# The entry of the first feed-forward block: the norm's weight moved behind the transposes, products ordered by weight tile

## The chip, the core and the metric

The kernel runs on one core of a Trainium2 chip. The metric is the device time of one execution in microseconds (us). Before the change the median of three runs is 1098.65 us (1098.41 to 1099.42).

## What is computed

The reference sends 256 tokens of 1024 channels through a block of feed-forward, attention and feed-forward parts, and then through two more layers. Only its first step matters here, the gate and up projections of the first feed-forward part behind its norm:

```python
def _rmsnorm(x, g):
    xf = x.astype(jnp.float32)
    r = lax.rsqrt(jnp.mean(xf * xf, axis=-1, keepdims=True) + EPS)
    return (xf * r * g.astype(jnp.float32)).astype(x.dtype)

def _swiglu(x, w_gate, w_up, w_down):
    return (jax.nn.silu(x @ w_gate) * (x @ w_up)) @ w_down
...
        f = _swiglu(_rmsnorm(x, ffn1_pre_g[l]), ffn1_w_gate[l], ffn1_w_up[l], ffn1_w_down[l])
```

Everything is float32.

## The kernel before

A float32 product is made of three products of a narrower type (float32r). Each operand is split into a high part, its cast, and a low part, the rest, and high x high, high x low and low x high are added up in PSUM. For weights, `Stream` does this: `load_to` (L68) issues 512 KB tiles on SP's queue into four raw buffers (`wraw`), `copy_next` (L77) casts a tile to `wh` (on ACT at L89, or on DVE at L87) and returns a function that makes `wl` (L94) on the engine it is given; a raw buffer is free, and the next load issued, when its low part is done. `copy_next` is called in program order; every engine works through its own instructions strictly in the order written here by hand.

Tokens come in two halves of 128. For each, `ew` (L386) has the squares summed (`rms`, L327: ACT at L336, then two small POOL operations for the scale r at L344 and L346) and writes `xs` = x times r times the norm's weight (DVE, L423). `to_t` (L362) transposes it in eight 128x128 pieces on PE (L370, against the identity `ident`), copies the result out of PSUM to the high part `xh` (ACT, L373) and returns the function that makes the low part `xl` (DVE, L378).

`setup` (L275) issues the loads: the tokens' first half, three weight tiles, the second half and a fourth tile on SP's queue; the norm's weight as one row on ACT's queue; `ident` and the table of small constants `small` on POOL's queue. PE runs `WARM` = 5 products of zeros (L300), then spreads the row over 128 partitions by products with a column of ones (L304, names `grow`), and DVE reads it from PSUM.

`enter_first` (L490) orders the entry of the first block. The first projection's weights are four tiles of two 128-row pieces (`w_first`: gate and up columns side by side, 512 wide). The inner function `first` of `ffn` (L631) makes the 24 products of one token half in one PSUM bank (`fh`, L642): for each tile high x high and high x low, at the end the eight low x high. The first half's 24 products stand first, with the second half's transposes before the last four of them; then the second half's 24. Behind them `gemm_b2` (L525) begins the next stage, products named `gb` (L535, L537).

Of the kernel before, what the change touches and what calls it, by code (L numbers as in the profile page):

```python
# [32 lines left out]

NB_RAW = 4
NB_HL = 6
WARM = 5


SM = {}
_o = 0  # L40
for _n, _w in (("convw", 16), ("convb", 4), ("ba", 4), ("bx", 4), ("lam", 4), ("glub", 4),
               ("lr", 16), ("li", 16), ("ldt", 16), ("d", 16)):
    SM[_n] = (_o, _w)
    _o += _w
NSM = _o

GAINS = ("ffn1_pre_g", "ffn1_post_g", "mix_pre_g", "mix_post_g", "ffn2_pre_g", "ffn2_post_g",
         "ab_norm_2", "ffn_norm_2_0", "cd_norm_2", "ffn_norm_2_1", "final_norm_2")


class Stream:
# [53 lines left out]
    def used(self):  # L105

        self.free = self.nt

    def take(self, n, used=True):
        if used:  # L110
# [78 lines left out]
class Kern:  # L189
# [85 lines left out]
    def setup(self):  # L275
        nc, A = self.nc, self.A
        nc.scalar.preload_act_table_set("silu_and_others")
        self.x = self.const.tile([P, 2, D + 4], F32, name="x")
        nc.gpsimd.memset(self.x[:, :, D:D + 1], 32.0 * math.sqrt(EPS))

        def load_x(h):
            for c in (slice(0, 512), slice(512, D)):
                nc.sync.dma_start(out=self.x[:, h, c], in_=A["x"][128 * h:128 * h + 128, c])

        load_x(0)
        self.ws.load_to(3)
# [5 lines left out]
        nc.vector.memset(t[:, 256:384], 1.0)  # L292
        warm = t[:, 0:256].bitcast(BF16)
        g = self.pre_of(0)
# [12 lines left out]
        nc.gpsimd.dma_start(out=self.ident, in_=A["c_ident"])  # L307
        self.mhalf = self.const.tile([P, 16], F32, name="mhalf")
        nc.gpsimd.memset(self.mhalf, -0.5)
        self.small = self.const.tile([P, NSM], F32, name="small")  # L310
        nc.gpsimd.dma_start(out=self.small, in_=A["smalls"])
        if self.phases[0] != "f1":
            for _ in self.s5_powers():
                pass
            for _ in self.rg_prep():
                pass

    def sv(self, name, i=None, n=1):
        o, w = SM[name]
        return self.small[:, o:o + w] if i is None else self.small[:, o + i:o + i + n]  # L320
# [41 lines left out]
    def to_t(self, h, src, oh, ol, n=8):  # L362

        nc = self.nc
        lo = []
        for b in range(0, n, 4):
            p = self.ps("tp")
            m = min(4, n - b)
            for j in range(m):
                nc.tensor.transpose(p[:, j * P:(j + 1) * P], src[:, (b + j) * P:(b + j + 1) * P], self.ident)  # L370
            pv = p[:, :m * P].rearrange("p (a t) -> p a t", a=m)
            hv = oh[:, b:b + m, h * P:(h + 1) * P]
            nc.scalar.copy(out=hv, in_=pv)  # L373
            lo.append((ol[:, b:b + m, h * P:(h + 1) * P], pv, hv))

        def low():
            for o, pv, hv in lo:
                nc.vector.tensor_sub(out=o, in0=pv, in1=hv.bitcast(F32))  # L378

        return low  # L380

# [4 lines left out]
    def ew(self, h, gname):  # L386

        nc = self.nc
        c2 = (slice(0, 512), slice(512, D))
        xv = self.x[:, h, :]  # L390
        xs = self.tmp.tile([P, D + 4], F32, name="xs", tag="xs")

        t = self.tmp.tile([P, D + 1], F32, name="pt", tag="pt", bufs=1)
        xsq = self.rms((xv[:, 0:512], xv[:, 512:D + 1]), t, 1.0 / 32)
        accs, gpost, coef = self.fin or (None, None, None)
        if gpost:
            acc = accs[h]
# [91 lines left out]

    def enter_first(self, e0, e1, first):  # L490

        V, G = self.nc.vector, self.nc.gpsimd
        for _ in range(3):
            next(e0)
        self.ws.copy_next()(G)
        xs = next(e0)
        self.ws.copy_next(V)(V)
        next(e1)
        next(e1)
        self.new_xt()  # L500
        low = self.to_t(0, xs, self.xh, self.xl)
        split = self.ws.copy_next()
        low()
        split(V)
        next(e1)
        self.ws.copy_next()(V)
        xs = next(e1)
        self.ws.ahead = 4
        first(0, lambda: self.to_t(1, xs, self.xh, self.xl)())
        self.ws.ahead = NB_HL  # L510
        self.ws.split_to(NB_HL)
        first(1, None)


    def mm3(self, out, prods, start, stop, late=False, mid=None):
# [99 lines left out]
    def ffn(self, gpre, gpost, coef, gnext, hooks=None, cut=False):  # L615
        nc = self.nc
        tt = nc.vector.tensor_tensor
        with self.tc.tile_pool(name="ffn", bufs=3) as fp:
# [5 lines left out]
            st = {}  # L624
            accs = None

            def act(c):
                hh, hl = hts[c // 2]
                return hh[:, c % 2, :], hl[:, c % 2, :]

            def first(h, mid):  # L631
                if h == 0:
# [10 lines left out]
                sg = fp.tile([P, S], F32, name="sgf", tag="sgf", bufs=2)  # L643
                nc.scalar.activation(out=sg, in_=p[:, 0:S], func=AF.Silu)
                tt(out=sg, in0=sg, in1=p[:, S:2 * S], op=ALU.mult)
                st[h] = sg

            def split(t, j):
                hh = fp.tile([P, 2, S], F32R, name="hh", tag="hh")
# [17 lines left out]
            for j in range(1, 11):  # L667
                sg = fp.tile([P, 2, S], F32, name="sg", tag="sg", bufs=1)
# [3 lines left out]
                if j == 1:  # L672
                    p = self.ps("ft")
# [1028 lines left out]
def _layout(inputs):  # L1702

    import numpy as np
    g = {k: np.asarray(v) for k, v in inputs.items()}
    A = {n: g[n] for n in _RAW}
# [8 lines left out]
    for n in GAINS:  # L1715
# [7 lines left out]
    q, k = g["q_norm_g"][0], g["k_norm_g"][0]  # L1723
    A["gqk"] = np.stack([q, sw(q), k, sw(k)])
    ch = lambda a: a.reshape(4, P).T
    st = lambda a: a.reshape(16, 2, 64).transpose(1, 2, 0).reshape(P, 16)
# [6 lines left out]
        "d": np.tile(g["cd_d_2"][0].reshape(16, 32).T, (4, 1)),  # L1733
# [27 lines left out]
```

## Time and profile before

| | |
|---|---|
| median of three runs | 1098.65 us |
| the profiled execution, its own time | 1100.22 us |
| its span, first to last instruction | 1098.4 us |
| PE busy | 1082.7 us, 99% of the span |
| DVE, ACT, POOL busy | 738.0, 598.3, 314.6 us |
| start of the next stage's first product (L535) | 27.35 us into the span |

The page gives shares of the whole span; a change that touches the first 28 us is read from the timeline of this stretch. In a timeline row the first number is the start in us from the span's start, the second the length, then engine, line, operation and tiles; "x8" means eight of them merged, and what stands in brackets is the idle time of the engine before it and what ended that. Matmul records overlap: the pace is the distance of their starts, not their length.

### The profile page before, as it was taken

What the parts mean: (1) busy time and instruction counts of PE and PEld (TensorE: products, weight loads), DVE (VectorE), ACT (ScalarE), POOL (GpSimd) and SP (SyncE); (2) the same over time, 40 slices, a digit from 0 to 9 for tenths busy, and PEclk for the clock granted to TensorE, in tenths of its full rate; (3) what the DMA queues carried; (4) which work ended last, traced back from release to release, by engine and by line L of the source; (5) the groups of instructions that cost most, each with busy time, mean ns of one, the idle gap of its engine ahead of it and who ended that gap; (6) DMA issues with size and microseconds to landing.
All of it is one profiled execution on the core that took longest, in us unless ns stands there. A gap on an engine that the chain in (4) does not pass through costs nothing.

```text
span 1098.4 us, 16117 instructions
## 1 busy us (share of the span) xinstructions
PE 1082.7 (99%) x5963; PEld 921.1 (84%) x5963; DVE 738.0 (67%) x1019; ACT 598.3 (54%) x954; POOL 314.6 (29%) x561
## 2 busy tenths in 40 slices
PE   8999999999999999999999999999999999999997
PEld 5888888878878888888987888888889888888886
DVE  5665676889676665667764676757777557565564
ACT  4667555556556554556575554545553465554553
POOL 4005840213310000003023599999505100000000
PEclk9999999999999999999999999999999999999999
DMA  7765565562056655655713665565454346656651
GB/s 237 252 203 179 193 206 176 188 217 75 20 159 226 207 176 193 208 175 185 225 54 100 212 202 177 172 202 181 158 180 160 106 132 196 207 167 203 206 168 63
DMA packets 130256, 190.83 MB, mean 174 GB/s; under 512 B 6017, under 2 KB 101249, under 8 KB 130178
## 3 DMA queue, kind: packets, MB, share of 16 engines
q1 hardware_dynamic: 129440, 187.72, 53.2%
q0 software_dynamic: 736, 2.08, 0.7%
q8 instruction: 47, 0.77, 0.3%
q14 instruction: 31, 0.25, 0.1%
q10 hardware_dynamic: 2, 0.00, 0.0%
HBM read 188.73 MB, written 1.05 MB: 173 GB/s over the span
## 4 chain that ended last, share of the span: by engine, by line
PE 89%; DVE 5%; issue 2%; ACT 1%; POOL 1%; DMA 1%; SPq 0%; POOLq 0%; DVEq 0%; ACTq 0%
PE gb L535 26%; PE f L523 21%; PE gb L537 13%; PE wo L523 5%; PE gb L523 5%; PE fh L642 4%; PE gh L523 3%; PE ga L523 2%; DVE wl L94 1%; PE tp L370 1%; PE lg L523 1%; PE o L888 1%; DMA wraw<-in_w_first_dram 1%; PE M L1382 1%; PE lt L1117 1%
## 5 line engine op out<-in xcount | busy, mean ns | idle before, releaser
L94 DVE TENSOR_TENSOR wl<-wraw,wh 128x1024 fp32r<-128x1024 f32 x338 | 411.6, 1258 | 105.5 <-ACT wh L89 104.4
L535 PE MATMUL gb<-xt,wh 128*128 128x512 f32 x1280 | 439.2, 390 | 0.0
L89 ACT CAST wh<-wraw 128x1024 fp32r<-128x1024 f32 x341 | 345.0, 1047 | 53.6 <-PE f L523 11.3
L537 PE MATMUL gb<-xt,wl 128*128 128x256 f32 x1280 | 353.9, 277 | 0.0
L535 PEld LDWEIGHTS gb<-xt,wh 128*128 128x128 f32 x1280 | 240.3, 188 | 50.7
L537 PEld LDWEIGHTS gb<-xt,wl 128*128 128x128 f32 x1280 | 240.4, 188 | 1.8
L523 PE MATMUL f<-wh,hh 128*128 128x512 f32 x348 | 138.2, 397 | 0.0
L523 PE MATMUL f<-wh,hl 128*128 128x512 f32 x348 | 137.1, 394 | 0.0
L523 PE MATMUL f<-wl,hh 128*128 128x512 f32 x348 | 136.9, 393 | 0.0
L659 ACT COPY sg<-gb 128x256 f32<-128x256 f32 x80 | 29.9, 373 | 142.6 <-PE gb L537 142.5
L660 DVE TENSOR_TENSOR sg<-gb,sg 128x256 f32<-128x256 f32 x80 | 33.2, 422 | 92.2 <-ACT sg L659 91.9
L344 POOL TENSOR_TENSOR v<-ss 128x1 f32<-128x1 f32 x22 | 6.6, 302 | 290.0 <-ACT xs L336 180.8
L523 PEld LDWEIGHTS f<-wh,hl 128*128 128x128 f32 x348 | 65.3, 188 | 16.9 <-DVE hl L654 0.9
L523 PEld LDWEIGHTS f<-wh,hh 128*128 128x128 f32 x348 | 65.4, 188 | 14.6
L523 PEld LDWEIGHTS f<-wl,hh 128*128 128x128 f32 x348 | 65.4, 188 | 13.3
L339 POOL TENSOR_SCALAR ss<-ss 128x1 f32<-128x1 f32 x6 | 2.4, 397 | 234.2 <-ACT xs L336 234.2
L523 PE MATMUL gb<-xt,wh 128*128 128x256 f32 x384 | 69.5, 283 | 0.0
L659 ACT COPY su<-gb 128x256 f32<-128x256 f32 x80 | 29.3, 368 | 65.7 <-PE gb L537 65.7
L523 PEld LDWEIGHTS gb<-xt,wh 128*128 128x128 f32 x384 | 59.4, 189 | 0.4
L523 PE MATMUL gb<-xt,wl 128*128 128x256 f32 x192 | 54.2, 282 | 0.0
L523 PE MATMUL wo<-wh,xt 128*128 128x512 f32 x160 | 52.5, 399 | 0.0
L653 ACT CAST hh<-sg 128x512 fp32r<-128x512 f32 x40 | 24.8, 621 | 50.8 <-DVE sg L680 50.8
(402 smaller groups left out, 1595.1 us busy)
## 6 DMA issues: line engine op xcount, KB each, us to landing
wraw<-in_ffn_w_down_dram SPq DMA_DIRECT2D x88, 512.0 KB, 3.9
wraw<-in_ffn_w_gate_dram SPq DMA_DIRECT2D x80, 512.0 KB, 4.1
wraw<-in_ffn_w_up_dram SPq DMA_DIRECT2D x80, 512.0 KB, 5.5
wraw<-in_ab_w_in_dram SPq DMA_DIRECT2D x20, 512.0 KB, 4.8
wraw<-in_w_qkv_dram SPq DMA_DIRECT2D x18, 512.0 KB, 3.8
wraw<-in_w_first_dram SPq DMA_DIRECT2D x16, 512.0 KB, 4.1
wraw<-in_cd_w_in_dram SPq DMA_DIRECT2D x16, 512.0 KB, 4.2
wraw<-in_w_out_dram SPq DMA_DIRECT2D x8, 512.0 KB, 3.5
```

The costliest lines, as they stand in the source:

```text
L89: self.nc.scalar.copy(out=h, in_=r)
L94: eng.tensor_tensor(out=l, in0=r, in1=h.bitcast(F32), op=ALU.subtract)
L370: nc.tensor.transpose(p[:, j * P:(j + 1) * P], src[:, (b + j) * P:(b + j + 1) * P], self.ident)
L523: self.nc.tensor.matmul(out=out, lhsT=l, rhs=r, start=start and i == 0, stop=stop and i == n - 1)
L535: self.nc.tensor.matmul(out=p, lhsT=wh[:, k % 4, c], rhs=self.x2[:, k, :], start=k == 0, stop=False, skip_group_check=True)
L537: self.nc.tensor.matmul(out=p[:, S:2 * S], lhsT=wl[:, k % 4, c], rhs=self.xh[:, k, :], start=False, stop=k == 7, skip_group_check=True)
L642: nc.tensor.matmul(out=p, lhsT=l, rhs=r, start=n == 0, stop=n == 23)
L653: nc.scalar.copy(out=hh, in_=t)
L659: nc.scalar.copy(out=t[:, c, :], in_=p[:, 1, :])
L660: tt(out=t[:, c, :], in0=p[:, 0, :], in1=t[:, c, :], op=ALU.add)
L888: nc.tensor.matmul(out=o, lhsT=v, rhs=p, start=i % 2 == 0 and n == 0, stop=i % 2 == 1 and n == 5)
L1117: nc.tensor.matmul(out=p[:, 0:384], lhsT=tri[:, 0, :], rhs=s, start=True, stop=False, skip_group_check=True)
```

## The change

The norm's weight no longer enters `xs`, which is now x times r (the new branch in `ew`). It is stored in `small` (eight columns `g1`, one factor per channel), and `to_t` applies it after the transposes, where a channel is a partition: the two 128x512 copies to `xh` and the two 128x512 subtractions to `xl` of each half become eight 128x128 operations each, with a factor per partition. The row's load and its products (L304) are gone. `ident` and `small` are loaded on ACT's queue. On SP's queue the second token half stands before the third weight tile.

PE runs 15 products of zeros at the start, and 4, 3 and 5 more at three later places. The 24 + 24 products are written out by tile: `put(h, i, x)` makes the two products of token half h and tile i, with x = 0 for high x high, 1 for high x low, 2 for low x high. `early` gives the tile before it is counted as taken.

```diff
-WARM = 5
+WARM = (15, 4, 3, 5)
...
-               ("lr", 16), ("li", 16), ("ldt", 16), ("d", 16)):
+               ("lr", 16), ("li", 16), ("ldt", 16), ("d", 16), ("g1", 8)):
...
         load_x(0)
-        self.ws.load_to(3)
+        self.ws.load_to(2)
         load_x(1)
         self.ws.load_to(NB_RAW)
...
-        row = self.g_p.tile([P, D], F32, name="grow", tag="g")
-        i = GAINS.index(g)
-        nc.scalar.dma_start(out=row[0:1, :], in_=A["gains"][i:i + 1, :])
-        p = self.ps("warm")
-        for _ in range(WARM):
-            nc.tensor.matmul(out=p, lhsT=warm[:, 0:P], rhs=warm, start=True, stop=True)
-        self.gains[g] = []
-        for c in (slice(0, 512), slice(512, D)):
-            p = self.ps("grow")
-            nc.tensor.matmul(out=p, lhsT=t[0:1, 256:384], rhs=row[0:1, c], start=True, stop=True)
-            self.gains[g].append(p)
+        self.wz = t[:, 0:256].bitcast(BF16)
+        self.wp = self.ps("warm")
+        self.warm(WARM[0])
         self.ident = self.const.tile([P, P], F32, name="ident")
-        nc.gpsimd.dma_start(out=self.ident, in_=A["c_ident"])
+        nc.scalar.dma_start(out=self.ident, in_=A["c_ident"])
...
-        nc.gpsimd.dma_start(out=self.small, in_=A["smalls"])
+        nc.scalar.dma_start(out=self.small, in_=A["smalls"])
...
+            for j in range(m):
+                g = gain[:, b + j:b + j + 1]
+                nc.scalar.activation(out=hv[:, j, :], in_=pv[:, j, :], func=AF.Copy, scale=g)
+                lo.append((ol[:, b + j, h * P:(h + 1) * P], pv[:, j, :], hv[:, j, :], g))
...
+                if g:
+                    nc.vector.scalar_tensor_tensor(out=o, in0=pv, scalar=g[0], in1=hv.bitcast(F32), op0=ALU.mult,
+                                                   op1=ALU.subtract)
...
+        if not self.fin:
+            r = next(xsq)
+            yield
+            for c in c2:
+                nc.vector.tensor_scalar(out=xs[:, c], in0=xv[:, c], scalar1=r, scalar2=None, op0=ALU.mult)
+            yield xs
+            return
...
     def enter_first(self, e0, e1, first):
...
+        self.new_xt()
+        low = self.to_t(0, xs, self.xh, self.xl, gain=g)
+        self.warm(WARM[1])
+        lo = ws.copy_next(V)
+        low()
+        put = first(None, None)
+        put(0, 0, 0)
+        lo(V)
+        put(0, 0, 2)
+        put(0, 0, 1)
+        lo = ws.copy_next()
...
+        put(0, 1, 0)
+        lo(V)
+        put(0, 1, 2)
+        put(0, 1, 1)
+        lo = ws.copy_next()
         next(e1)
+        self.warm(WARM[2])
+        xs = next(e1)
+        put(0, 2, 0)
+        lo(V)
+        put(0, 2, 2)
+        self.warm(WARM[3])
+        low = self.to_t(1, xs, self.xh, self.xl, gain=g)
+        put(0, 2, 1)
+        lo = ws.copy_next()
+        lo(V)
+        put(0, 3, 0)
+        put(0, 3, 2)
+        for i in range(4):
+            put(1, i, 0)
         low()
+        put(0, 3, 1)
+        put(0, None, None)
+        for i in range(4):
+            put(1, i, 1)
+        ws.take(4)
+        for i in range(4):
+            put(1, i, 2)
+        put(1, None, None)
```

How the order of instructions moves is seen at three places. The first is PE, from the first half's products to the next stage; `fh_206` and `fh_260` are the banks of the first and the second token half before the change:

```order
23 L642 MATMUL fh_206<-wh,xt 128x512 x4
24 L642 MATMUL fh_260<-wh,xt 128x512 x2
25 L642 MATMUL fh_260<-wl,xt 128x512 x2
26 L642 MATMUL fh_260<-wh,xt 128x512 x2
27 L642 MATMUL fh_260<-wl,xt 128x512 x2
28 L642 MATMUL fh_260<-wh,xt 128x512 x2
29 L642 MATMUL fh_260<-wl,xt 128x512 x2
30 L642 MATMUL fh_260<-wh,xt 128x512 x2
31 L642 MATMUL fh_260<-wl,xt 128x512 x2
32 L642 MATMUL fh_260<-wh,xt 128x512 x8
33 L535 MATMUL gb<-xt,wh 128x512
```

With the change, the banks are `fh_193` and `fh_194`, and the same stretch begins with the second half's transposes:

```order
61 L370 MATMUL tp<-ident,xs 128x128 x8
62 L691 MATMUL fh_193<-wl,xt 128x512 x2
63 L691 MATMUL fh_193<-wh,xt 128x512 x4
64 L691 MATMUL fh_194<-wh,xt 128x512 x8
65 L691 MATMUL fh_193<-wl,xt 128x512 x2
66 L691 MATMUL fh_194<-wl,xt 128x512 x8
67 L691 MATMUL fh_194<-wh,xt 128x512 x8
68 L578 MATMUL gb<-xt,wh 128x512
```

Row 63 holds the first four products that need the fourth tile. From them on thirty products remain, and the second half's products of all four tiles are among these.

The second place is ACT, from the second half's squares (`pt,ss<-x`) on. Before the change the fourth tile's cast stands ahead of the copies to `xt`:

```order
8 L336 ACTIVATE pt,ss<-x 128x512
9 L336 ACTIVATE pt,ss<-x 128x513
10 L89 CAST wh<-wraw 128x1024
11 L373 CAST xt<-tp 128x4x128 x2
12 L644 ACTIVATE sgf<-fh_206 128x256
```

With the change the second and the third tile's casts (row 7) stand ahead of the squares, and the fourth tile's behind the copies:

```order
6 L379 ACTIVATE xt<-tp,small 128x128 x8
7 L89 CAST wh<-wraw 128x1024 x2
8 L335 ACTIVATE pt,ss<-x 128x512
9 L335 ACTIVATE pt,ss<-x 128x513
10 L379 ACTIVATE xt<-tp,small 128x128 x8
11 L89 CAST wh<-wraw 128x1024
12 L676 ACTIVATE sgf<-fh_193 128x256
```

The first tile's cast has left ACT for DVE, where it was the second tile's before.

The third place is DVE, from the first token half's scaling (`xs`) to the second's. Before:

```order
3 L423 SCALAR_TENSOR_TENSOR xs<-x,r,grow 128x512 x2
4 L87 CAST wh<-wraw 128x1024
5 L94 TENSOR_TENSOR wl<-wraw,wh 128x1024
6 L378 TENSOR_TENSOR xt<-tp,xt 128x4x128 x2
7 L94 TENSOR_TENSOR wl<-wraw,wh 128x1024 x2
```

With the change:

```order
2 L426 TENSOR_SCALAR xs<-x,r 128x512 x2
3 L87 CAST wh<-wraw 128x1024
4 L385 SCALAR_TENSOR_TENSOR xt<-tp,small,xt 128x128 x8
5 L94 TENSOR_TENSOR wl<-wraw,wh 128x1024 x2
6 L426 TENSOR_SCALAR xs<-x,r 128x512 x2
7 L94 TENSOR_TENSOR wl<-wraw,wh 128x1024 x2
```

The tokens' low parts now stand ahead of the first weight low part, which POOL made before; the second half's scaling stands ahead of the third tile's low part.

## Rows read from the trace of the kernel before

**Rows 1.** The page: busy time of PE; the chain that ended last, by engine.

```profile
PE 1082.7 (99%) x5963; PEld 921.1 (84%) x5963; DVE 738.0 (67%) x1019; ACT 598.3 (54%) x954; POOL 314.6 (29%) x561
...
PE 89%; DVE 5%; issue 2%; ACT 1%; POOL 1%; DMA 1%; SPq 0%; POOLq 0%; DVEq 0%; ACTq 0%
```

**Rows 2.** Timeline of PE and its weight loads (PEld), 0 to 28 us.

```profile
2.02 0.15 PEld L300 LDWEIGHTS <-warm 128*128 128x128 bf16 x1 [0.28 <-issue]
...
2.45 0.15 PEld L300 LDWEIGHTS <-warm 128*128 128x128 bf16 x1 [0.28 <-issue]
...
3.44 3.78 PE L304 MATMUL grow<-grow,warm 1*128 1x512 f32 x4
...
7.14 2.03 PE L370 MATMUL tp<-ident,xs 128*128 128x128 f32 x8
...
12.50 1.22 PE L642 MATMUL fh<-wl,xt 128*128 128x512 f32 x2 [0.77 <-POOL wl L94]
...
20.00 1.04 PE L370 MATMUL tp<-ident,xs 128*128 128x128 f32 x8
...
25.50 2.01 PE L642 MATMUL fh<-wh,xt 128*128 128x512 f32 x8
...
27.35 0.39 PE L535 MATMUL gb<-xt,wh 128*128 128x512 f32 x1
```

**Rows 3.** Timeline of ACT, DVE and POOL, same stretch.

```profile
5.25 0.56 POOL L346 TENSOR_TENSOR r<-v,mhalf 128x1 f32<-128x1 f32 x1
...
8.93 1.04 ACT L89 CAST wh<-wraw 128x1024 fp32r<-128x1024 f32 x1 [4.04 <-DMA wraw<-in_w_first_dram]
...
9.88 1.07 ACT L373 CAST xt<-tp 128x512 fp32r<-128x512 f32 x2
...
10.05 2.40 POOL L94 TENSOR_TENSOR wl<-wraw,wh 128x1024 fp32r<-128x1024 f32 x1 [4.24 <-ACT wh L89]
...
10.27 2.74 DVE L87 CAST wh<-wraw 128x1024 fp32r<-128x1024 f32 x1 [2.27 <-DMA wraw<-in_w_first_dram]
...
11.58 1.04 ACT L89 CAST wh<-wraw 128x1024 fp32r<-128x1024 f32 x1 [0.64 <-DMA wraw<-in_w_first_dram]
...
12.54 0.62 ACT L336 ACTIVATE pt<-x 128x512 f32<-128x512 f32 x1
...
14.18 1.28 DVE L378 TENSOR_TENSOR xt<-tp,xt 128x512 fp32r<-128x512 f32 x2
...
14.39 0.56 POOL L346 TENSOR_TENSOR r<-v,mhalf 128x1 f32<-128x1 f32 x1
...
15.38 2.35 DVE L94 TENSOR_TENSOR wl<-wraw,wh 128x1024 fp32r<-128x1024 f32 x2
...
27.83 4.05 ACT L89 CAST wh<-wraw 128x1024 fp32r<-128x1024 f32 x4
```

**Rows 4.** Groups by line and form: count, busy us, mean ns of one.

```profile
L87 DVE CAST wh<-wraw 128x1024 fp32r<-128x1024 f32 x3 | 4.1, 1370 | 2.3 <-DMA wraw<-in_w_first_dram 2.3
...
L421 DVE TENSOR_SCALAR xs<-xs,r 128x512 f32<-128x512 f32 x6 | 2.6, 484 | 2.2 <-POOL r L346 2.2
...
L785 DVE TENSOR_TENSOR val<-ga,vah 128x128 fp32r<-128x128 f32 x2 | 0.6, 292 | 0.7 <-ACT vah L784 0.7
...
L450 ACT ACTIVATE xs<-xg,r 128x512 f32<-128x512 f32 x2 | 1.4, 722 | 2.5 <-POOL r L346 2.5
...
L671 ACT ACTIVATE sg<-sg 128x512 f32<-128x512 f32 x40 | 25.3, 632 | 21.2 <-DVE sg L660 21.2
...
L784 ACT CAST vah<-ga 128x128 fp32r<-128x128 f32 x2 | 0.5, 267 | 2.7 <-DVE qa L782 2.7
```

**Rows 5.** Windows: busy us by engine; last three columns: granted clock, DMA share, GB/s.

```profile
10.00:11.00 1.00, 0.49 (x1) 0.49 (x2) 0.73 (x1) 0.95 (x2) 0.95 (x1) 1.00 1.02 395
11.50:12.50 1.00, 0.23 (x1) 0.00 (x0) 1.00 (x1) 0.92 (x1) 0.95 (x1) 1.00 0.14 53
12.50:13.40 0.90, 0.90 (x2) 0.80 (x3) 0.86 (x2) 0.90 (x4) 0.00 (x0) 1.00 0.14 52
```

More of the change, by code (lines that the diff above doesn't have):

```diff
@@ L107, in used, with early @@
         self.free = self.nt
+    def early(self, i):
+        h, l = self.hl[i]
+        a = self.specs[i][1][0]
+        return h.rearrange("p (a b) -> p a b", a=a), l.rearrange("p (a b) -> p a b", a=a)
     def take(self, n, used=True):
@@ L291, in setup @@
         nc.vector.memset(t[:, 0:256], 0.0)
-        nc.vector.memset(t[:, 256:384], 1.0)
-        warm = t[:, 0:256].bitcast(BF16)
-        g = self.pre_of(0)
-        row = self.g_p.tile([P, D], F32, name="grow", tag="g")
-        i = GAINS.index(g)
-        nc.scalar.dma_start(out=row[0:1, :], in_=A["gains"][i:i + 1, :])
-        p = self.ps("warm")
-        for _ in range(WARM):
-            nc.tensor.matmul(out=p, lhsT=warm[:, 0:P], rhs=warm, start=True, stop=True)
-        self.gains[g] = []
-        for c in (slice(0, 512), slice(512, D)):
-            p = self.ps("grow")
-            nc.tensor.matmul(out=p, lhsT=t[0:1, 256:384], rhs=row[0:1, c], start=True, stop=True)
-            self.gains[g].append(p)
+        self.wz = t[:, 0:256].bitcast(BF16)
+        self.wp = self.ps("warm")
+        self.warm(WARM[0])
         self.ident = self.const.tile([P, P], F32, name="ident")
-        nc.gpsimd.dma_start(out=self.ident, in_=A["c_ident"])
+        nc.scalar.dma_start(out=self.ident, in_=A["c_ident"])
         self.mhalf = self.const.tile([P, 16], F32, name="mhalf")
@@ L316, in setup, with warm @@
                 pass
+    def warm(self, n):
+        for _ in range(n):
+            self.nc.tensor.matmul(out=self.wp, lhsT=self.wz[:, 0:P], rhs=self.wz, start=True, stop=True)
     def sv(self, name, i=None, n=1):
@@ L360, in new_xt, with to_t @@
         self.xh, self.xl = (t[:, o:o + 8 * S].rearrange("p (a t) -> p a t", a=8) for o in (oh // 4, ol // 4))
-    def to_t(self, h, src, oh, ol, n=8):
+    def to_t(self, h, src, oh, ol, n=8, gain=None):
         nc = self.nc
@@ L372, in to_t @@
             hv = oh[:, b:b + m, h * P:(h + 1) * P]
-            nc.scalar.copy(out=hv, in_=pv)
-            lo.append((ol[:, b:b + m, h * P:(h + 1) * P], pv, hv))
-        def low():
-            for o, pv, hv in lo:
-                nc.vector.tensor_sub(out=o, in0=pv, in1=hv.bitcast(F32))
+            if gain is None:
+                nc.scalar.copy(out=hv, in_=pv)
+                lo.append((ol[:, b:b + m, h * P:(h + 1) * P], pv, hv))
+                continue
+            for j in range(m):
+                g = gain[:, b + j:b + j + 1]
+                nc.scalar.activation(out=hv[:, j, :], in_=pv[:, j, :], func=AF.Copy, scale=g)
+                lo.append((ol[:, b + j, h * P:(h + 1) * P], pv[:, j, :], hv[:, j, :], g))
+        def low():
+            for o, pv, hv, *g in lo:
+                if g:
+                    nc.vector.scalar_tensor_tensor(out=o, in0=pv, scalar=g[0], in1=hv.bitcast(F32), op0=ALU.mult,
+                                                   op1=ALU.subtract)
+                else:
+                    nc.vector.tensor_sub(out=o, in0=pv, in1=hv.bitcast(F32))
         return low
@@ L490, in enter_first @@
     def enter_first(self, e0, e1, first):
-        V, G = self.nc.vector, self.nc.gpsimd
+        V, ws = self.nc.vector, self.ws
+        g = self.sv("g1")
         for _ in range(3):
             next(e0)
-        self.ws.copy_next()(G)
         xs = next(e0)
-        self.ws.copy_next(V)(V)
+        self.new_xt()
[9 more added lines that the diff above has]
+        lo = ws.copy_next()
         next(e1)
         next(e1)
-        self.new_xt()
-        low = self.to_t(0, xs, self.xh, self.xl)
-        split = self.ws.copy_next()
-        low()
[L504 to L512, printed above, removed]
+        put(0, 1, 0)
[3 more added lines that the diff above has]
+        lo = ws.copy_next()
+        next(e1)
+        self.warm(WARM[2])
[12 more added lines that the diff above has]
+            put(1, i, 0)
+        low()
+        put(0, 3, 1)
[6 more added lines that the diff above has]
+        put(1, None, None)
     def mm3(self, out, prods, start, stop, late=False, mid=None):
@@ L629, in act, with shut, parts, put @@
                 return hh[:, c % 2, :], hl[:, c % 2, :]
+            def shut(h, p):
+                sg = fp.tile([P, S], F32, name="sgf", tag="sgf", bufs=2)
+                nc.scalar.activation(out=sg, in_=p[:, 0:S], func=AF.Silu)
+                tt(out=sg, in0=sg, in1=p[:, S:2 * S], op=ALU.mult)
+                st[h] = sg
+            def parts():
+                banks, n, w = [self.ps("fh0"), self.ps("fh1")], [0, 0], {}
+                def put(h, i, x):
+                    if i is None:
+                        return shut(h, banks[h])
+                    if i not in w:
+                        w[i] = self.ws.early(i)
+                    t = slice(h * P, (h + 1) * P)
+                    for k in range(2):
+                        nc.tensor.matmul(out=banks[h], lhsT=(self.xl if x == 2 else self.xh)[:, 2 * i + k, t],
+                                         rhs=w[i][x == 1][:, k, :], start=n[h] == 0, stop=n[h] == 23)
+                        n[h] += 1
+                return put
             def first(h, mid):
+                if h is None:
+                    return parts()
                 if h == 0:
@@ L642, in first @@
                     nc.tensor.matmul(out=p, lhsT=l, rhs=r, start=n == 0, stop=n == 23)
[L643 to L646, printed above, removed]
+                shut(h, p)
             def split(t, j):
@@ L1732, in _layout @@
         "ldt": st(np.repeat(g["cd_log_dt_2"][0][:, None], 64, 1)),
-        "d": np.tile(g["cd_d_2"][0].reshape(16, 32).T, (4, 1)),
+        "g1": g["ffn1_pre_g"].reshape(8, P).T, "d": np.tile(g["cd_d_2"][0].reshape(16, 32).T, (4, 1)),
     }
```

## The prediction, made before the change was run

> **What bounds the kernel now.** I read the page first: PE is busy for 99% of the span and holds 89% of the chain that ended last [rows 1]. Everything behind the first projection runs at PE's pace, and the change edits nothing there, so it can only move the moment at which that dense part starts. The end of the stage is the first product of the next one (the first gb row of L535), at 27.35 us [rows 2]. Whatever moves this moment moves the end of the run.
>
> The timeline of PE up to there shows two things [rows 2]. First, its pace. The loads between the five zero products of L300 start at 2.02 and 2.45, 0.43 us apart, and at 25.50 eight products of the same width take 2.01 us, 0.23 each: the lower and the upper of the two clock levels. The change-over lies a little before 19 us; the eight transposes from 20.00 take 1.04 us, those from 7.14 took 2.03. (The page's clock row reads full speed there too; the pace is what I go by.) PE was occupied from 1.19 to 9.2 us by the zero products, the four one-row passes of L304 and eight transposes, and that did not raise the clock. Second, its waits: at 12.50, for instance, for the low part of the first weight tile.
>
> The timelines of the other engines say why [rows 3]. ACT and DVE wait for weights to land: the casts at 8.93, 10.27 and 11.58 are each released by a transfer. POOL takes 2.40 us for the first low part, and the DVE cast beside it 2.74, where three such casts average 1370 ns [rows 4], so the other two took (3 x 1.37 - 2.74) / 2 = 0.69: the two engines held each other up. The second token half starts late (squares at 12.54, its scale at 14.39).
>
> The windows of the transfers show that the landings are late because of few engines [rows 5]. Until 11.0 the DMA share is 1.02; from 11.5 to 13.4 it is 0.14 of sixteen, about two engines still at work. Each transfer counts as landed with its last engine, so weights and tokens land up to 1.9 us after the other fourteen engines are done. ident and small, the only transfers of POOL's queue there, went through in the microseconds in which these two fell behind. That is a coincidence in one trace, not a proof.
>
> **The change part by part, case A (my forecast).** Times are from the span's start.
>
> *Transfers.* ident and small go from POOL's queue to ACT's; the gain row's transfer goes, eight columns join small. On SP's queue the second token half passes ahead of the third weight tile, which lands where the token half did. I take it that the two engines no longer trail and the landings come 1.9 us sooner: first tile 7.0 instead of 8.93, third in the token half's old place, 12.9 - 1.9 = 11.0. The bounds are no gain (case B) and this gain. ACT issues two transfers instead of one before its first square; it waits for tokens then, so nothing. The 118 KB of ident and small (64 and 54, by their shapes) now run beside the first tokens; at 395 GB/s [rows 5] that is 0.3 us on the first scale, and the wait for the first weights at 7.0 covers it, and twice as much.
> The Trainium skill (DMA: Bandwidth & Descriptors, Issuing engines are not separate DMA queues) speaks against any gain: transfers run on the same 16 engines whoever issues them. By it alone the landings stay, which is case B's sum. The same page (Latency and other measured facts) says that two of the engines are usually slower, with descriptor traffic of GpSimd's queue as a best guess; by that the delay goes with the queue, and case B would have 1 in 10. No run here shows either yet.
>
> *First scale.* The gain's product leaves the normalization: xs is now a scaling at 0.48 us a half [rows 4] instead of 0.75, and no longer waits for L304. With the scale ready at 5.25 + 0.56 = 5.81 [rows 3], xs is there at 6.3 and 6.7.
>
> *PE before the weights.* Fifteen zero products instead of five: from 1.19, ten at 0.43 and, if the clock has risen by then, five at 0.22: until 6.6. I take this because ten solid products are full-width work such as preceded the rise before 19 us; the bounds are 6.4 us at the lower pace for all (until 7.6) and the early rise. Transposes 8 x 0.11 (seven steps from 20.00 and a last one of 0.27 make the 1.04): until 7.5. Four zero products: until 8.4, beside waiting, so free.
>
> *Transposed tokens, high part (ACT).* Two copies of 128x512 (1.07 us the pair, [rows 3]) become eight of 128x128 with a factor per partition. Lower bound: 0.13 each, an eighth of the pair. Upper: 0.27 for such a copy plus 0.09 for the factor (722 against 632 ns), 0.36 [rows 4]. I take the middle, 0.25, so 2.0 us per token half, 0.95 more than before, from 7.25 to 9.25.
>
> *Low part (DVE).* Two of 128x512 (1.28 the pair, [rows 3]) become eight of 128x128: between 0.16 and 0.29 each [rows 4]; I take 0.25, 2.0 us.
>
> *Weights.* DVE casts the first tile without POOL beside it: 7.0 to 7.7. Low token parts until 9.7, the first tile's low part (1.2, half of the pair at 15.38 [rows 3]) until 10.95, the second's until 12.1. POOL's 2.40 us are gone, but this puts the first low weight part behind eight small operations. ACT casts the second tile behind its copies, until 10.3, and the third from 11.0 to 12.0.
>
> *PE with weights.* First four products from 8.4; the next wait until 11.0 for the first low part; then eight at 0.23, three zero products, four products, five zero products: 1.85 + 0.65 + 0.93 + 1.08, until 15.5.
>
> *Second token half.* Its squares stand behind the third cast: 12.0. From square to scale took 14.39 + 0.56 - 12.54 = 2.41 before, so 14.4, and xs at 14.9. PE is ready for the transposes at 15.5 only, so the eight zero products cost about 0.6 here. The first four transposes are out at 16.1; the eight copies until 18.15.
>
> *The new wait.* ACT's cast of the fourth tile is queued behind these copies: 18.15 to 19.2, though the tile lands much earlier. PE, in order, waits for it from about 17 (2.2 us) with the second half's products of the first three tiles standing behind. Thirty products remain: 30 x 0.2315 = 6.95.
>
> *Sum.* 19.2 + 6.95 = 26.15 against 27.35 [rows 2]: 1.2 us sooner. Behind it, the loads of later raw tiles wait for low parts: the fourth ends at 20.4 now, where it ended at 15.38 + 2.35 = 17.73 [rows 3]. The casts of those tiles began at 27.83 before, behind the stage's own end, and are needed one group of products later; that covers it, and without the cover it would be up to 2.7 us. The profiled execution took 1100.22, so 1099.0 in its terms; the median of the runs lies 1.57 below that execution, so 1098.65 - 1.2 = **1097.45**.
>
> *Addresses.* small grows by 32 bytes a partition and everything behind it moves by as much; no distance between tiles changes. The trace has no two placements of one product to compare. I cost it at nothing, since the distances stay; a nanosecond on some 4,700 wide products would be 4.7 us either way.
>
> **The rivals.**
> *B, the landings stay.* For it: the bytes ahead of the third tile do not shrink. Against: only two engines trailed. First tile 8.93, low part of the tokens until 11.65, first low weight part 12.85, eight products until 14.7, the rest until 17.35 (zero products included, which now cost where PE is late); copies 18.0 to 20.0, cast until 21.05, end 28.0: 0.65 later, 1099.3.
> *C, the other side: the clock does not rise on zero products.* For it: eight occupied microseconds did not raise it before [rows 2]. Against: most of these were one-row passes and transposes. Its place is the pace of PE from 7 to 18 us. At the lower level until 18.7: fifteen until 7.6, transposes 9.3, four 11.0, four products 12.7, eight 16.1, three 17.4, four 19.1, five 20.2, copies from 20.85, cast until 23.9, end 30.85: 3.5 later, 1102.1. It decides if the pace is still 0.43 beyond about 12 us; below that the landings hide it.
> *D, small operations are cheap.* With 0.16 and 0.18 instead of 0.25, an earlier rise and the same landings, each ACT group is 0.7 shorter and DVE's 0.55: end about 25.05, 2.3 sooner, 1096.35.
> *E, the shift of addresses counts,* either way, by 2 us or more.
>
> **How the numbers follow.** A 0.46, D 0.20, B 0.16, C 0.11, E 0.07. About 0.2% (2.2 us) is what a measurement of this kernel can tell from no change: faster means below 1096.45, slower above 1100.85. Faster: a little over half of D (0.12; it lies at the bound), 0.03 of A and half of E, 0.18. Slower: most of C (0.07; where the clock rises in between it costs less) and half of E, 0.10. The same: 0.72. The range, 1095.6 to 1100.2, holds A, B and D with the bounds of the small operations; C's upper part and E lie outside.
>
> **What would show it.** Right: L370's first transposes start near 6.6 and take 0.11 each; the first cast on DVE takes 0.7 and starts near 7.0; the DMA share falls from one to nothing without two engines trailing; ACT's eight copies take 2.0 per half; PE waits some 2.2 us for the fourth cast; the first product of the next stage stands near 26.2. Wrong: a first cast near 8.9 (B), products 0.43 apart beyond 12 us (C), copies at 0.16 (D), or another pace in the dense part (E). A forecast of the sum fails most easily on the landings and on the copies.

## The result, and the profile after

The changed kernel takes 1105.41 us (median of 4, 1104.92 to 1106.10) where the kernel before takes 1098.85 beside it (1098.41 to 1099.42): ratio 1.0065, 95% interval 1.0053 to 1.0077, 6.56 us slower. Forecast: 1097.45, in 1095.6 to 1100.2. The prediction was wrong, and in its sign.

First the page of the changed kernel: busy times, then the dense part (line, operation, count, busy us, mean ns).

```profile
PE 1083.2 (98%) x5981; PEld 921.8 (84%) x5981; DVE 740.7 (67%) x1031; ACT 600.6 (54%) x966; POOL 310.1 (28%) x558
...
L578 PE MATMUL gb<-xt,wh 128*128 128x512 f32 x1280 | 439.3, 390 | 0.0
```

The same group of the kernel before:

```profile
L535 PE MATMUL gb<-xt,wh 128*128 128x512 f32 x1280 | 439.2, 390 | 0.0
```

PE is as busy as before [rows 1] and the dense products take the same 390 ns. So the loss lies ahead of them. The timeline of that stretch:

```profile
1.19 4.82 PE L315 MATMUL warm<-warm 128*128 128x512 bf16 x15 [1.19 <-DVE warm L297]
...
6.67 1.09 PE L370 MATMUL tp<-ident,xs 128*128 128x128 f32 x8 [0.67 <-DVE xs L426]
7.27 0.69 DVE L87 CAST wh<-wraw 128x1024 fp32r<-128x1024 f32 x1 [0.25 <-DMA wraw<-in_w_first_dram]
7.37 2.18 ACT L379 ACTIVATE xt<-tp,small 128x128 fp32r<-128x128 f32 x8 [2.17 <-PE tp L370]
...
8.54 2.16 DVE L385 SCALAR_TENSOR_TENSOR xt<-tp,small,xt 128x128 fp32r<-128x128 f32 x8 [0.58 <-ACT xt L379]
...
11.32 1.05 ACT L89 CAST wh<-wraw 128x1024 fp32r<-128x1024 f32 x1 [0.85 <-DMA wraw<-in_w_first_dram]
...
11.89 0.73 PE L691 MATMUL fh<-wl,xt 128*128 128x512 f32 x2 [2.19 <-DVE wl L94]
...
12.28 0.63 ACT L335 ACTIVATE pt<-x 128x512 f32<-128x512 f32 x1
...
13.96 0.56 POOL L345 TENSOR_TENSOR r<-v,mhalf 128x1 f32<-128x1 f32 x1
...
14.55 5.90 DVE L426 TENSOR_SCALAR xs<-x,r 128x512 f32<-128x512 f32 x2 [1.58 <-POOL r L345]
...
16.31 0.65 POOL L777 MEMSET vah<- 128x640 f32 x1
...
16.53 0.60 PE L370 MATMUL tp<-ident,xs 128*128 128x128 f32 x4
...
18.77 1.39 POOL L777 MEMSET vbl<- 128x1536 f32 x1
...
20.51 0.66 PE L370 MATMUL tp<-ident,xs 128*128 128x128 f32 x4 [3.38 <-DVE xs L426]
21.20 1.14 ACT L379 ACTIVATE xt<-tp,small 128x128 fp32r<-128x128 f32 x4 [2.89 <-PE tp L370]
...
22.22 1.06 ACT L89 CAST wh<-wraw 128x1024 fp32r<-128x1024 f32 x1
...
23.33 5.15 PE L691 MATMUL fh<-wh,xt 128*128 128x512 f32 x12 [0.47 <-ACT wh L89]
...
32.48 0.39 PE L578 MATMUL gb<-xt,wh 128*128 128x512 f32 x1
```

Two rows are not as forecast. The two scalings of the second token half (L426) take 5.90 us where the first half's take 0.88; they end at 20.45, just behind POOL's last memset (18.77 + 1.39 = 20.16): POOL clears four buffers for a later stage there. The chain of waits (start, length, engine and tile) puts nearly all of it on the second one:

```profile
14.95 5.51 DVE xs L426
```

And the twelve products from 23.33 take 5.15 us, some 0.43 each, the clock's lower level; eight from 25.50 took 2.01 before [rows 2], 0.23 each, the upper level. The windows show it too (columns: stretch, length, busy us of PE and count, granted clock, DMA share, GB/s):

```profile
17.00:20.40 3.40, 0.13 (x2) 1.00 0.46 165
...
23.30:28.30 5.00, 4.97 (x12) 0.53 0.59 191
```

Theory L: POOL's memsets hold up the scaling, because of its new form (one input tile where it had two). Theory C: PE's waits let the clock fall, and that costs on top of it. Rivals: the scaling waits for something else (M); the new order of the work costs the time (N).

### The profile page after: what moved, and what is told of

Its sections match the earlier page's. It is cut to its first block, busy times and chain, and to the rows that moved or that the text cites. A ratio compares the mean times of both kernels' runs of the same rounds, so it can differ in the third digit from the quotient of the medians.

```text
span 1103.6 us, 16175 instructions
## 1 busy us (share of the span) xinstructions
PE 1083.2 (98%) x5981; PEld 921.8 (84%) x5981; DVE 740.7 (67%) x1031; ACT 600.6 (54%) x966; POOL 310.1 (28%) x558
## 4 chain that ended last, share of the span: by engine, by line
PE 89%; DVE 5%; ACT 2%; issue 2%; POOL 1%; DMA 1%; SPq 0%; POOLq 0%; DVEq 0%; ACTq 0%
PE gb L578 26%; PE f L566 21%; PE gb L580 13%; PE wo L566 5%; PE gb L566 5%; PE gh L566 3%; PE fh L710 3%; PE ga L566 2%; DVE wl L94 1%; PE tp L370 1%; PE fh L691 1%; PE lg L566 1%; PE o L953 1%; DMA wraw<-in_w_first_dram 1%; PE M L1447 1%
## 5 line engine op out<-in xcount | busy, mean ns | idle before, releaser
L94 DVE TENSOR_TENSOR wl<-wraw,wh 128x1024 fp32r<-128x1024 f32 x339 | 412.8, 1257 | 110.9 <-ACT wh L89 109.9
```

Of the source, the lines that this page charges most:

```text
L94: eng.tensor_tensor(out=l, in0=r, in1=h.bitcast(F32), op=ALU.subtract)
```

## The experiments

Times are medians; the ratio is to the kernel before, run beside it.

**POOL's work moved away (e1_pool_clear).** The memsets go to the start, the three transfers to SP's queue.

```diff
-        nc.gpsimd.dma_start(out=self.rope, in_=A["c_rope"])
+        nc.sync.dma_start(out=self.rope, in_=A["c_rope"])
...
-        for t in self.va + self.vb:
-            nc.gpsimd.memset(t.bitcast(F32), 0.0)
...
                 self.m1_open(stm)
+                for t in self.va + self.vb:
+                    self.nc.gpsimd.memset(t.bitcast(F32), 0.0)
```

> The changed kernel with POOL's work taken out of the stretch: the four memsets of m1_load move to the start (POOL is idle there until 5.27), its three transfers go from POOL's queue to SP's. Theory L: the second token half's scaling (one input, SBUF to SBUF) was held by POOL's work, 5.50 us instead of 0.48. Then both scalings are done by 15.5, the clock doesn't fall back, the fourth cast comes behind the copies at about 18.5, the first gb product stands at 26.5 instead of 32.48, and the time is 1105.4 - 6.0 = 1099.4. Rival M: the scaling waits for something else that its record takes in (its own turn on DVE, a transfer); then it still takes over 5 us and the time stays at 1105. Rival N: most of the loss is the order of work (zero products ahead of the transposes, the fourth cast behind the copies) and the clock's fall; then the scaling gets short but the first gb product stays beyond 29 and the time above 1102.

1103.60, ratio 1.0044 (1.0027 to 1.0061). Its timeline:

```profile
12.95 1.91 PE L691 MATMUL fh<-wh,xt 128*128 128x512 f32 x4
...
14.55 0.88 DVE L426 TENSOR_SCALAR xs<-x,r 128x512 f32<-128x512 f32 x2 [1.29 <-POOL r L345]
...
18.40 1.04 PE L370 MATMUL tp<-ident,xs 128*128 128x128 f32 x8
...
22.20 4.60 PE L691 MATMUL fh<-wh,xt 128*128 128x512 f32 x12 [2.29 <-ACT wh L89]
...
30.79 0.39 PE L578 MATMUL gb<-xt,wh 128*128 128x512 f32 x1
```

The scaling takes 0.88: M falls, and POOL's work is what held it. But only 1.8 of the expected 6.0 us came back. From 12.5 to 15.9 and from 22.8 to 26.2 the products run at the lower pace (four from 12.95 in 1.91; they take 1.08 in the changed kernel); the granted clock reads 0.50 from 13 to 15 and from 23 to 25. Each time PE had waited: the starts ahead lie 2.60 and 2.69 us apart.

**Only the memsets moved (e2_sets_early).** The transfers stay on POOL's queue.

```diff
-        for t in self.va + self.vb:
-            nc.gpsimd.memset(t.bitcast(F32), 0.0)
...
                 self.m1_open(stm)
+                for t in self.va + self.vb:
+                    self.nc.gpsimd.memset(t.bitcast(F32), 0.0)
```

> e1_pool_clear, but m1_load's three transfers stay on POOL's queue; only the four memsets move to the start. In the changed kernel the second scaling was held from 14.95, while POOL's first memset began at 16.31. If issuing transfers holds DVE up too, the two scalings take until about 16.4 (1.8 instead of 0.88); if only memsets do, 0.88. The time is that of e1_pool_clear (1103.6) either way, since PE reaches the transposes at 18.4 there.

1103.34, ratio 1.0040 (1.0025 to 1.0055).

```profile
15.24 0.90 DVE L426 TENSOR_SCALAR xs<-x,r 128x512 f32<-128x512 f32 x2 [1.81 <-POOL r L345]
...
15.92 0.56 POOL L774 DMA_DIRECT2D gqk<-in_gqk_dram  x1
```

The issue of transfers beside it does nothing: the memsets hold the scaling.

**The scaling with two inputs (e3_two_inputs),** POOL's work left in place.

```diff
-        nc.vector.memset(t[:, 0:256], 0.0)
+        nc.vector.memset(t[:, 0:512], 0.0)
+        self.wzf = t[:, 0:512]
...
-                nc.vector.tensor_scalar(out=xs[:, c], in0=xv[:, c], scalar1=r, scalar2=None, op0=ALU.mult)
+                nc.vector.scalar_tensor_tensor(out=xs[:, c], in0=xv[:, c], scalar=r, in1=self.wzf, op0=ALU.mult, op1=ALU.add)
```

> The changed kernel with the scaling as a two-input operation (times the scale, plus a tile of zeros in SBUF); POOL's memsets and transfers stay where they are. If it is the one-input form that POOL's work holds up (theory L), each scaling takes about 0.70 (as the two-input scaling of the kernel before did beside the same memsets), xs is there at 16.0, the first gb product at about 26.6 and the time is 1099.5. If POOL's work holds up any operation of DVE between SBUF and SBUF, the second one still takes about 5 us and the time stays at 1105.

1104.08, ratio 1.0045 (1.0030 to 1.0060).

```profile
14.65 1.41 DVE L427 SCALAR_TENSOR_TENSOR xs<-x,r,warm 128x512 f32<-128x512 f32 x2 [1.05 <-POOL r L346]
...
15.98 1.22 DVE L94 TENSOR_TENSOR wl<-wraw,wh 128x1024 fp32r<-128x1024 f32 x1
...
16.42 0.65 POOL L778 MEMSET vah<- 128x640 f32 x1
```

Not held, 0.71 each; so it is the form. By these records both scalings were done (16.06) before the first memset began; what is compared is the place, since the one-input scaling stood from 14.95 on in the changed kernel, also ahead of the first memset. The low part behind them (L94, two inputs in SBUF) ran beside the memsets in its usual 1.22. The expected 1099.5 was missed: the end stays late for the same reason as in the first run, the clock falls behind both waits.

**The kernel before with one input (e4_before_one_input).** The kernel leaves the norm's weight out here, so its output differs.

```diff
+            elif not self.fin:
+                nc.vector.tensor_scalar(out=xs[:, c], in0=xv[:, c], scalar1=r, scalar2=None, op0=ALU.mult)
```

> The kernel before with its first scaling in the one-input form (the gain is left out of the first norm, so the output differs); nothing else changes. Theory L: the scalings issued at 17.64 can't pass POOL's two long memsets (17.73 to 20.45); the second ends at about 20.9 where it ended at 19.04, the transposes that began at 20.00 end some 0.5 to 1.4 later, and the time is 1099.4 to 1100.3 instead of 1098.85. Rival M: both take 0.48 and the time is that of the kernel before.

1100.41, ratio 1.0017 (1.0008 to 1.0026).

```profile
16.92 3.48 DVE L423 TENSOR_SCALAR xs<-x,r 128x512 f32<-128x512 f32 x2
17.00 1.40 POOL L714 MEMSET vbh<- 128x1536 f32 x1
...
18.33 1.39 POOL L714 MEMSET vbl<- 128x1536 f32 x1
...
20.06 1.09 PE L370 MATMUL tp<-ident,xs 128*128 128x128 f32 x8 [1.17 <-DVE xs L423]
```

One edited branch brings the hold into the kernel before, and 1.9 us with it. The first of the two scalings takes 3.09 and ends at 20.01, behind the last memset's end at 19.72; the second takes 0.47.

**The waits filled, the scaling still held (e5_fill).** Fifteen zero products between the transposes, four before the last tile.

```diff
+            if b:
+                self.warm(fill)
...
-        low = self.to_t(1, xs, self.xh, self.xl, gain=g)
+        low = self.to_t(1, xs, self.xh, self.xl, gain=g, fill=15)
...
+        self.warm(4)
         put(0, 3, 0)
```

> The changed kernel with fifteen more zero products between the second half's two groups of transposes and four more ahead of the fourth tile's first product, where PE waited. The scaling stays held until 20.45. If the lower clock behind these waits costs what the pace says (eleven products at 0.427 instead of 0.2315, 2.15 us), the products from 23.33 run 0.23 apart, the first gb product stands at about 30.4 and the time is 1103.3. If the clock falls all the same, or wasn't what stretched them, it stays at 1105.4.

1104.88, ratio 1.0054 (1.0039 to 1.0069).

```profile
15.12 5.91 DVE L428 TENSOR_SCALAR xs<-x,r 128x512 f32<-128x512 f32 x2 [1.61 <-POOL r L345]
...
25.12 3.03 PE L694 MATMUL fh<-wh,xt 128*128 128x512 f32 x12 [0.82 <-ACT wh L89]
```

The twelve products take 3.03 instead of 5.15, so the fill works; but in this execution the clock had already fallen behind the earlier wait (from 13.8), and the filling stood in the way of the last four transposes (22.35, though the scaling ended at 21.03; 20.51 in the changed kernel), so only 0.5 of 2.15 us arrived. The expectation held for the pace and missed for the end.

**Both: POOL cleared and waits filled (e6_clear_fill).** Ten zero products in each of the two long waits.

```diff
         put(0, 0, 2)
+        self.warm(10)
         put(0, 0, 1)
...
         put(0, 2, 1)
+        self.warm(10)
```

> e1_pool_clear with ten zero products in each of the two long waits that PE had there (ahead of the first low weight part, 9.58 to 12.18, and ahead of the fourth tile, 19.51 to 22.20). Theory C: TensorE's clock goes back to its lower level because PE stands still there; in e1_pool_clear seven products from 12.53 and eight from 22.78 ran 0.43 apart instead of 0.23, and the zero products between them too. Filled, nothing behind 7 runs at the lower pace, the copies of the second half start near 16.4 instead of 19.04, the first gb product stands at 26.5 to 27 instead of 30.79 and the time is 1099.5. If the clock falls for another reason (a level that goes up and down by itself at the start), the products stay at 0.43 and the time at 1103.6 or above.

1100.14, ratio 1.0013 (1.0003 to 1.0022).

```profile
16.58 1.04 PE L370 MATMUL tp<-ident,xs 128*128 128x128 f32 x8
...
19.23 1.09 ACT L89 CAST wh<-wraw 128x1024 fp32r<-128x1024 f32 x1
...
20.38 3.03 PE L693 MATMUL fh<-wh,xt 128*128 128x512 f32 x12
```

No product behind 7 us runs at the lower pace (the granted clock reads 1.00 from there on), and the first gb product stands at 27.38. The four runs together:

| | waits open | waits filled |
|---|---|---|
| scaling held | 1105.41 | 1104.88 |
| scaling free | 1103.60 | 1100.14 |

Alone the two cures give 1.8 and 0.5, together 5.3: with the hold gone, PE loses at the lower clock much of what it no longer waits; with the hold in place, the filling itself kept the last transposes back. The two fills are not the same (e5_fill leaves the wait ahead of the first low weight part open), so the table is no exact crossing of two causes.

**Another order (e7_order),** POOL cleared, no zero products behind the first nineteen.

```diff
-        lo = ws.copy_next(V)
+        ws.copy_next(V)(V)
         low()
...
         lo = ws.copy_next()
-        next(e1)
-        next(e1)
+        for _ in range(3):
+            next(e1)
         put(0, 1, 0)
...
+        lo = ws.copy_next()
         low = self.to_t(1, xs, self.xh, self.xl, gain=g)
+        put(0, 2, 2)
         put(0, 2, 1)
-        lo = ws.copy_next()
         lo(V)
```

> e1_pool_clear in another order, with no zero products behind the first nineteen: the first tile's low part goes ahead of the eight low token parts on DVE, the second half's squares ahead of the third cast on ACT, the fourth cast ahead of the second half's copies, the second half's transposes behind two products of the third tile on PE. By the durations of the changed kernel's rows no wait of PE is over 1.1 us then and the first gb product stands at 22.2, 8.6 earlier than in e1_pool_clear: 1095.0, under the kernel before (1098.5). If the clock falls all the same, ten to twenty products take 0.2 more each: 24 to 26, 1097 to 1099. If the order doesn't matter, 1103.6.

1095.18, ratio 0.9969 (0.9956 to 0.9981): 3.7 us below the kernel before, faster than both.

```profile
8.19 1.23 DVE L94 TENSOR_TENSOR wl<-wraw,wh 128x1024 fp32r<-128x1024 f32 x1
...
12.18 2.03 ACT L89 CAST wh<-wraw 128x1024 fp32r<-128x1024 f32 x2
...
13.34 0.89 DVE L426 TENSOR_SCALAR xs<-x,r 128x512 f32<-128x512 f32 x2 [0.72 <-POOL r L345]
...
15.98 2.92 PE L687 MATMUL fh<-wh,xt 128*128 128x512 f32 x12
...
22.88 0.39 PE L574 MATMUL gb<-xt,wh 128*128 128x512 f32 x1
```

The first low part is made at 8.19 (at 10.62 in the changed kernel), both casts of ACT stand before the copies; no two starts of PE from 7 us on lie over 0.9 us apart, and the clock stays up. So the order does matter, as N said, but it was not N alone:

**The same order with POOL's work back in place (e11_order_held).** To e7_order:

```diff
                 self.m1_open(stm)
-                for t in self.va + self.vb:
-                    self.nc.gpsimd.memset(t.bitcast(F32), 0.0)
...
-        nc.sync.dma_start(out=self.rope, in_=A["c_rope"])
+        nc.gpsimd.dma_start(out=self.rope, in_=A["c_rope"])
...
+        for t in self.va + self.vb:
+            nc.gpsimd.memset(t.bitcast(F32), 0.0)
```

> e7_order with POOL's memsets and transfers of m1_load where the changed kernel has them. The second half's scaling starts at 13.3 here. Theory L: its second operation is held until the last memset ends, near 19.0, with thirty-four products and four transposes of PE behind it; the first gb product stands at 27.5, or at 29 to 29.5 if the clock falls in the wait as well: 1099.8 to 1101.8, all of e7_order's gain and more. If the order alone gets round the hold, 1095.2.

1102.57, ratio 1.0036 (1.0024 to 1.0048).

```profile
13.64 5.90 DVE L426 TENSOR_SCALAR xs<-x,r 128x512 f32<-128x512 f32 x2 [0.72 <-POOL r L345]
...
17.86 1.39 POOL L773 MEMSET vbl<- 128x1536 f32 x1
...
19.59 1.11 PE L370 MATMUL tp<-ident,xs 128*128 128x128 f32 x4 [4.76 <-DVE xs L426]
...
29.27 0.39 PE L574 MATMUL gb<-xt,wh 128*128 128x512 f32 x1
```

This is 0.8 above the expected range. The hold, with nothing to hide it, is worth 7.4 us; the clock's fall is in it (PE's starts lie 0.43 apart from 20.9 to 22.2).

**The new order with five zero products (e9_few_zero).** To e7_order:

```diff
-WARM = (15, 4)
+WARM = (5, 0)
```

> e7_order with five zero products (as the kernel before had) instead of nineteen. If the zero products are what brings TensorE's clock up in time, PE runs at 0.43 a product until 16 to 18.5 (the kernel before: 18.7), the first gb product moves from 22.88 to 24.2 to 25.0 and the time from 1095.2 to 1096.5 to 1097.3. If the waits for weights hide the lower pace, or the first products themselves raise the clock by 12, 1095.2.

1095.53, ratio 0.9970 (0.9958 to 0.9982): the same as with nineteen.

```profile
6.86 1.97 PE L370 MATMUL tp<-ident,xs 128*128 128x128 f32 x8 [3.35 <-DVE xs L426]
...
10.33 2.36 PE L687 MATMUL fh<-wh,xt 128*128 128x512 f32 x6
```

The transposes and the first products run at the lower pace, the clock rises within these six products (11.8), and the waits that follow take the difference in. The fourteen zero products left out are worth nothing in this order.

**The transfers' queue, from both sides.** To the changed kernel (e8_pool_queue):

```diff
-        nc.scalar.dma_start(out=self.ident, in_=A["c_ident"])
+        nc.gpsimd.dma_start(out=self.ident, in_=A["c_ident"])
...
-        nc.scalar.dma_start(out=self.small, in_=A["smalls"])
+        nc.gpsimd.dma_start(out=self.small, in_=A["smalls"])
```

> The changed kernel with ident and small back on POOL's queue, nothing else. If POOL's queue makes two of the sixteen engines trail, as the prediction took it, the first weight tile lands near 8.9 (7.24 in the changed kernel) and the third near 12.9 (11.30), and the first gb product comes 1 to 2 later: 1106.5 to 1107.5. If the landings came sooner for another reason, they stay at 7.2 and 11.3 and the time at 1105.4.

1105.09, ratio 1.0060 (1.0045 to 1.0075). The first cast starts at 8.78, released by its transfer, as the theory of the trailing engines had it, but the time is that of the changed kernel. In its trace two things offset each other:

```profile
24.70 3.02 PE L691 MATMUL fh<-wh,xt 128*128 128x512 f32 x12 [0.97 <-ACT wh L89]
```

The fourth cast ends at 24.64, 1.4 later than in the changed kernel, but PE waits less ahead of these products (its starts lie at most 1.35 apart from 13.55 on), the clock is at its upper level, and thirty products take 7.0 instead of 9.15; the first gb product stands at 31.69. So the equal time does not show that late landings cost nothing. In the kernel before, the opposite edit (e10_before_queue):

```diff
-        nc.gpsimd.dma_start(out=self.ident, in_=A["c_ident"])
+        nc.scalar.dma_start(out=self.ident, in_=A["c_ident"])
...
-        nc.gpsimd.dma_start(out=self.small, in_=A["smalls"])
+        nc.scalar.dma_start(out=self.small, in_=A["smalls"])
```

> The kernel before with ident and small issued from ACT's queue, nothing else: this part of the change alone. If transfers of POOL's queue delay the landings (e8_pool_queue: first tile 8.76 instead of 6.6 to 8.0), the first two tiles land near 7 and 8.5, some 1.5 sooner, and about 1 to 1.5 of it reaches the end: 1097.2 to 1097.9. If the later waits of that stage hide it, the time is that of the kernel before.

1097.96, ratio 0.9992 (0.9983 to 1.0001): inconclusive, at most 1.9 us. Its first cast is at 8.09.

**The kernel before, once more (e12_before_again),** with no edit.

> The kernel before, once more, for a second trace. Its profiled execution was 1100.22 beside a median of 1098.65, and the prediction carried that difference over to the changed kernel, whose profiled execution lies at its median. If the difference was that execution's own (weights that landed late), an execution near 1098.6 shows the first two casts before 8.93 and 10.27 and the first gb product near 25.8. If profiling itself costs 1.5, it comes out at 1100.2 with 27.35 again.

1098.88, ratio 0.9998 (0.9988 to 1.0008); the profiled execution has a span of 1096.8.

```profile
7.59 1.05 ACT L89 CAST wh<-wraw 128x1024 fp32r<-128x1024 f32 x1 [2.56 <-DMA wraw<-in_w_first_dram]
...
16.33 1.40 DVE L423 SCALAR_TENSOR_TENSOR xs<-x,r,grow 128x512 f32<-128x512 f32 x2
...
16.41 1.40 POOL L712 MEMSET vbh<- 128x1536 f32 x1
...
25.65 0.39 PE L535 MATMUL gb<-xt,wh 128*128 128x512 f32 x1
```

The 27.35 of [rows 2] was that one execution's; here it is 25.65 (26.16 in e10_before_queue, whose profiled execution took 1098.72). The two-input scaling with the gain in PSUM runs beside a memset in its usual time.

## Why the prediction was wrong, point by point

- **Up to the second half's scale it held, but for one term.** First tile 7.24 (7.0), eight copies 2.18 (2.0), low parts 2.16 (2.0), third cast 11.32 (11.0), squares 12.28 (12.0), scale 14.52 (14.4). The term that did not hold: the low parts of the tokens were forecast right behind DVE's cast, from 7.7, but waited for ACT's copies and began at 8.54. So PE got the first low weight part at 11.89 (11.0) and reached the transposes at 16.53 (15.5).
- **The step that failed is "xs at 14.9".** It added one scaling of 0.48, from rows where POOL was idle [rows 4], to 14.4, and a second would have ended by 15.4; the second ended at 20.45. The evidence stood in the prediction itself: the cast of 2.74 beside POOL's 2.40 [rows 3] is a one-input operation held beside POOL (0.69 in the changed kernel, without it). It was used to credit the cast that POOL left, and not to charge the scaling, which meets POOL's memsets before and after the change. The change had taken the second input out of the scaling together with the gain. The copies end at 22.34 (18.15) and the fourth cast at 23.28 (19.2), 4.1 late. Of this about 3.0 is the hold: in e6_clear_fill, without it and with the transposes at the same place (16.58), the fourth cast ends at 20.32. The other 1.1 is PE's lateness above and copies of 2.18 for 2.0.
- **The second is "thirty products x 0.2315 = 6.95".** They took 32.48 - 23.33 = 9.15, 2.2 more, at the clock's lower level behind the waits. The prediction had named the wait of 2.2 us for the fourth cast, and in rival C asked only whether the clock rises, not whether it falls again. In e6_clear_fill, without hold and with the waits filled, thirty products take 27.38 - 20.38 = 7.0 and the wait ahead of them, which the zero products fill from 17.93, lasts until 20.38, 2.45 for the forecast 2.2: these two terms were right. 3.0 + 1.1 + 2.2 = 6.3 is the whole distance from 26.15 to 32.48.
- **The base was off too.** "The median lies 1.57 below that execution" was carried over to the change. The difference belonged to that execution, whose weights landed late (first cast 8.93; 7.59 in e12_before_again, first gb product 1.70 sooner). Against that trace's 25.65 the sum's own 26.15 is 0.5 slower, not 1.2 faster: 1099.35. With every term of the sum in place the change would still have gained nothing; e6_clear_fill, without hold and lower clock, is slower than the kernel before too (1100.14). From 25.65 to 32.48 it is 6.83, for the 6.56 between the medians.
- **Landings (case A against B).** Not settled. With ident and small on POOL's queue the first cast that waits for its tile starts at 7.59, 8.20, 8.78 and 8.93 in four executions; on ACT's queue between 7.27 (the changed kernel) and 8.09 (e10_before_queue) in six. The spread of executions covers most of the difference, so that the first tile came close to its forecast may be chance; one engine pair that trails in one trace was too little to credit 1.9 us.
- **C** came in a shape not described: the clock rose at 4.1 and had fallen by 21.6. **D** fell (0.27 a copy). **E** fell (390 ns as before).
- **Of the zero products,** those at the start were credited with the early clock; e9_few_zero shows that in its order five do as well.

## What to carry to other kernels

A change that makes an operation cheaper can change which engines hold it up: price a one-input operation between SBUF tiles by what POOL does at the moment when it runs, and read that from the timeline, not from its mean. Where PE waits for other engines, the clock can fall back: either order the work so that the waits go (here worth 5 us more than filling them), or count some of the products behind each long wait at the lower level. And take the base of a sum from two traces before crediting anything that one of them shows as a late landing.

## What the runs showed of the hardware that had not been expected

- A one-input operation of DVE between SBUF tiles stands still while POOL clears buffers one after the other: 5.51 us for a scaling of 0.48 in the changed kernel, 3.09 for one beside the last memsets in e4_before_one_input. DVE got no turn between two memsets: in all five kernels with a hold (these two, e5_fill, e8_pool_queue, e11_order_held) the held scaling ends about 0.3 us behind the last memset. Operations with two inputs were not held beside memsets: 1.40 for the two scalings with the gain in PSUM (e12_before_again), 1.22 for a low part with both inputs in SBUF (e3_two_inputs). The Trainium skill (SBUF — State Buffer, SBUF: two separate sides) calls the port pair that DVE and GpSimd share an "exclusive lock, not a bandwidth split", taken by DVE operations in a two-port mode, which copies, casts and one-input scalings can enter; the trace agrees as to the form and the blocking, though no run shows the mode. By its rule the operation that starts first keeps the pair. Here the measurement differs: the row of the held scaling starts at 14.95, ahead of the first memset's at 16.31; transfers alone don't hold it (0.90 for two in e2_sets_early). What holds it in that first 1.4 us stays open.
- The clock falls and rises again within the first 30 us, and the same wait does not always bring it down: behind starts 2.60 us apart the changed kernel's execution kept the upper pace, e1_pool_clear fell to 0.43 within one product, and e5_fill after five products at the upper pace. With no two starts over 0.9 us apart (e7_order) it stayed up. What else decides it was not tried.
